# The low halves of all weights computed by VectorE alone

## The chip, the cores and the metric

The kernel runs on one core of one Trainium2 chip. The metric is the device time of one execution in microseconds (us); lower is better. The engines of the core have short names in the profile: PE is TensorE (PEld its weight loads), DVE is VectorE, ACT is ScalarE, POOL is GpSimd, SP issues the DMAs.

## The reference

One layer of a hybrid decoder, for a prompt of 2048 tokens and for 8 short sequences of 4 tokens that share the weights. All arrays are fp32, the model width is 1024:

```
h    = rmsnorm(x, norm1_g) * (1 + sc1) + sh1          # adaLN: sh, sc, g from silu(c) @ ada_w + ada_b
proj = h @ w_in                                       # columns split among three token mixers
mix  = concat(ssd(proj), rwkv7(proj), s5(proj)) @ w_out
x    = x + g1 * mix
h2   = rmsnorm(x, norm2_g) * (1 + sc2) + sh2
x    = x + g2 * (square(relu(h2 @ mlp_w1)) @ mlp_w2)  # 1024 -> 4096 -> 1024
y    = rmsnorm(x, final_g)
```

The mixers are a Mamba-2 SSD in chunks, an RWKV-7 time mixing and a complex-diagonal S5; their final states are outputs too. Only the four large products, with w_in, w_out, mlp_w1 and mlp_w2, use the weights that the change touches.

## The kernel before

Activations lie with features on the 128 partitions and tokens along the free axis. The prompt is cut into four blocks of 512 tokens (`NB`, `BT`); block `SB` = 2 carries the 32 sample tokens as 32 more columns. The input projection runs for all four blocks first; then, block by block, the output projection, and the MLP in chunks of four hidden tiles. The mixers' second stages are generators (`spawn`) that a planner (`pump`) fits between the matmuls, so most of the mixers' work lies beside the projections and the MLPs of blocks 0 and 1.

The large products keep fp32 accuracy by halves. TensorE multiplies in the rounded type fp32r, so each operand is split: a high half, the value rounded to fp32r, and a low half, the value minus its high half. A product is three matmuls per 128 x 128 weight block: high x high, high x low, low x high (the loop over `i` in `gemm` and `gemm2`). Accumulation is in a PSUM bank (`bk`).

The weights go through this stage by stage. `wload` brings a raw tile of 128 x 1024 into one of four buffers in `arena`. `wprep` lets ScalarE write the high half of 512 columns into a ring of four in `arena_r`; `wlow` writes the low half into the same slot of the ring: VectorE takes the first 512 - `WS.POOL` columns, GpSimd the other `WS.POOL`. `WS.POOL` is 288 (so 224 and 288 columns) for all input projections and for the output projection and MLP of blocks 0 and 1, and 0 from the output projection of block 2 on (line 2538). The first kind are the 176 halves of w_in and all but the last few of the 288 of blocks 0 and 1 in w_out, w1 and w2: the trace has 462. `whalf` and the middle of `gemm` (`k % 4 == 2`, one half ahead) call `wlow`, so the low half stands in VectorE's and GpSimd's queues among the mixers' instructions. Before each engine instruction stand the waits that the tile framework derives; each engine works through its queue in the order in which the program was written.

The order is written out by the program itself. Every instruction goes through `Eng.call` (line 198, which is why nearly all lines of the profile are L198), which issues it and then books it in `Plan`: `plan.run` moves the rough clock of its engine by an assumed cost (for a `tensor_tensor` of n columns, 72 + 1.04 n on VectorE and 60 + 2.4 n on GpSimd). `pump` looks at these clocks to choose which generator writes its next piece. GpSimd's other instructions are pieces of the mixers: subtractions and products of 504 or 512 columns and short copies.

Of the kernel before, what the change touches and what calls it, by code (L numbers as in the profile page):

```python
# [13 lines left out]
ALU = mybir.AluOpType  # L14
# [96 lines left out]


class Plan:
    """Rough clocks of the engines while the program is written; they only decide the order in which it is written."""

    LAT = {"PE": 197.0, "DVE": 128.0, "ACT": 143.0, "POOL": 85.0, "SP": 0.0}
    U = 32
# [130 lines left out]
def layer_kernel(ctx: ExitStack, tc: tile.TileContext, d, o, dbg=None):  # L248
    nc = tc.nc
    plan = Plan()  # L250
    V, S, P, T, Q = (Eng(plan, *x) for x in (("DVE", nc.vector), ("ACT", nc.scalar), ("POOL", nc.gpsimd), ("PE", nc.tensor), ("SP", nc.sync)))
# [31 lines left out]

    ctx.enter_context(tc.manual_schedule())

    # ------------------------------------------------------------ plumbing
    gens = []
    done = set()

# [146 lines left out]
    tt = V.tensor_tensor  # L436
# [11 lines left out]
    def bc(ap, k, n):  # L448
        return ap.unsqueeze(k).to_broadcast([*ap.shape[:k], n, *ap.shape[k:]])

    # ------------------------------------------------------------ constants
    cst = M.get(C_N)
    vec = M.get(V_N)
    cin = M1.get(72)
# [52 lines left out]
    s5dec = M.get(512)  # L507
    V.memset(s5h.f, 0.0)

    # ------------------------------------------------------------ small helpers  # L510
    def rsqrt(v, n, p=128):
        t_, y_, h_ = (grab(n, AM) for _ in range(3))
        t, y, h = t_.f[0:p], y_.f[0:p], h_.f[0:p]
        ts(t.bitcast(I32), v.bitcast(I32), 1, None, ALU.logical_shift_right)
        ts(h, v, -27.0 / 1024, None, ALU.mult)
        ts(y.bitcast(I32), t.bitcast(I32), -1.0, float(0x5F3759DF), ALU.mult, ALU.add)
        tt(t, y, y, ALU.mult)
        tt(t, t, v, ALU.mult)
        stt(t, t, -10.0 / 3, t, ALU.add, ALU.mult)
        yield 0  # L520
        stt(y, t, 5.0, y, ALU.add, ALU.mult)
        tt(t, y, y, ALU.mult)
        tt(t, t, h, ALU.mult)
        stt(y, t, 0.5625, y, ALU.add, ALU.mult)
        yield 0
        free(t_, h_)
        return y_
# [77 lines left out]
        ts(dv(D_A, 8), dv(D_A, 8), -1.0, None, ALU.mult)  # L605
        done.add("A")

    # ------------------------------------------------------------ adaLN
    mod = M.get(48 * 9)
    modv = mod.v("p (m s) -> p m s", m=48)  # L610
    G1 = M.get(72)
# [68 lines left out]
            yield  # L680
            yield from finish()

    # ------------------------------------------------------------ weights
    NWH = 4
    wring = [(MR.get(512), MR.get(512)) for _ in range(NWH)]
    wbuf = M.get(1024 * NRB)
# [3 lines left out]
    class WS:  # L690
# [4 lines left out]
        POOL = 288  # L695

    def wload(upto):
        while WS.loaded < min(upto, len(wseq)):
            i = WS.loaded
            dst = wraw[i % NRB]  # L700
            Q.dma_start(dst if wseq[i][1] != "oh" else dst.rearrange("p (m c) -> p m c", m=2), wseq[i][0])
            WS.loaded += 1

    def whalves(i):
        hi, lo = wring[i % NWH]
        return hi, lo, wraw[i // 2 % NRB][:, 512 * (i % 2):512 * (i % 2) + 512]
# [9 lines left out]
    def wlow(upto):  # L716
        while WS.low < min(upto, WS.ready):
            i = WS.low
            hi, lo, raw = whalves(i)
            c = 512 - WS.POOL  # L720
            tt(lo.r[:, 0:c], raw[:, 0:c], hi.f[:, 0:c], ALU.subtract)
            if c < 512:
                P.tensor_tensor(lo.r[:, c:], raw[:, c:], hi.f[:, c:], ALU.subtract)
            WS.low += 1
            wload(i // 2 + (NRB if i % 2 else NRB - 1))

    def whalf():
        i = WS.pos
        WS.pos += 1
        wprep(i + 3)  # L730
        wlow(i + 1)
        hi, lo = wring[i % NWH]
        return hi.r, lo.r
# [45 lines left out]
    def gemm(xs, hasS, drop=()):  # L779
        nk = len(xs)  # L780
        got, ws = [], []
        for (c0, c1) in pieces(hasS):
            bk = gbank()
            assert bk is not None
            n = c1 - c0
            cnt = 0
            for k in range(nk):
                if k % 4 == 0 and k // 4 == len(ws):
                    ws.append(whalf())
                if k % 4 == 2:  # L790
                    wlow(WS.pos + 2)
                hi, lo = ws[k // 4]
                xh, xl = xs[k]
                h_, l_ = hi[:, 128 * (k % 4):128 * (k % 4) + 128], lo[:, 128 * (k % 4):128 * (k % 4) + 128]
                for i, (w_, x_) in enumerate(((h_, xh), (h_, xl), (l_, xh))):
                    x_ = x_[:, c0:c1]
                    t = plan.when([w_, x_], "PE")
                    while t > plan.clk["PE"] + 150 and pump(t - plan.clk["PE"]):
                        pass
                    mm(bk[:, 0:n], w_, x_, start=cnt == 0, stop=cnt == nk * 3 - 1)  # L800
                    cnt += 1
                    if i == 2 and drop and c1 >= BT:
                        free(*drop[k])
                    if cnt % SLOT == 0 and cnt < nk * 3:
                        pump()
            got.append((bk, c0, c1))
        return got

    def gemm2(acts, hasS):
# [4 lines left out]
        for k in range(8):  # L814
            if k > 0 or not WS.pos:
                wait_for(lambda: len(acts) > k, "acts")
            if k == 0:
                pos = WS.pos
                wprep(pos + 2 * nt)
                wlow(pos + 2 * nt)  # L820
                WS.pos += 2 * nt
                wait_for(lambda: len(acts) > k, "acts")
            if k == 6:
                wprep(WS.pos + 1)
                wlow(WS.pos + 1)
            xh, xl = (x.r for x in acts[k])
            for u, (m, (c0, c1)) in enumerate(units):
                hi, lo = (w.r for w in wring[(pos + 2 * m + k // 4) % NWH])
                h_, l_ = hi[:, 128 * (k % 4):128 * (k % 4) + 128], lo[:, 128 * (k % 4):128 * (k % 4) + 128]
                for i, (w_, x_) in enumerate(((h_, xh), (h_, xl), (l_, xh))):  # L830
                    x_ = x_[:, c0:c1]
                    t = plan.when([w_, x_], "PE")
                    while t > plan.clk["PE"] + 150 and pump(t - plan.clk["PE"]):
                        pass
                    mm(bks[u][:, 0:c1 - c0], w_, x_, start=k + i == 0, stop=k == 7 and i == 2)
                    cnt += 1
                    if cnt % SLOT == 0 and cnt < 24 * len(units):
                        pump()
# [20 lines left out]
                fn(bk, BT - c0, c1 - c0, BT, True)  # L859
            gput(bk)  # L860

    # ------------------------------------------------------------ token mixers, first stage
    def store(dst, src):
        Q.dma_start(dst, src)

# [307 lines left out]
        ub.free()  # L1173
        done.add(("u", b, i))

    # ------------------------------------------------------------ S5
    LWS = -0.30326532985631671

    def s5_setup():
# [369 lines left out]
        yf.free()  # L1549
        done.add(("s5", b))  # L1550

    # ------------------------------------------------------------ SSD
    def ssd_chunk(b, c):
        smp = c == 4
        n = 32 if smp else 128
# [159 lines left out]
        for c in cs:  # L1715
            yield from admit(ssd_chunk(b, c), C_SSD, R_SSD(b))

    # ------------------------------------------------------------ RWKV, second stage
    def rw_pre(b):
        hasS = b == SB  # L1720
        nch = 9 if hasS else 8
# [370 lines left out]
        if b == SB:  # L2092
            spawn(ssd_gen(b, [4]), R_SMP)

    # ------------------------------------------------------------ main line
    def mix_flags(b):
        fl = [("s5", b)]
        for c in range(5 if b == SB else 4):
            fl += [("ssd", b, c), ("rw", b, c)]
        return fl  # L2100
# [403 lines left out]
        free(*xs)  # L2504
        done.add(("final", b))

    # ------------------------------------------------------------ run
    first4 = [4, 0, 5, 1, 6, 2, 7, 3]
    nxt = [[]]
    ys = []  # L2510
# [49 lines left out]
        dbg(nc, locals())  # L2560


# [1 line left out]
def _consts():  # L2564
    c = np.zeros((128, C_N), np.float32)
    i = np.arange(128)
    c[:, C_ID:C_ID + 128] = np.eye(128)
    c[:, C_MLE:C_MLE + 128] = i[:, None] <= i[None]
    c[:, C_MGT:C_MGT + 128] = i[:, None] > i[None]
    c[:, C_BD:C_BD + 128] = (i[:, None] // 64) == (i[None] // 64)  # L2570
    s, t = i[:, None] % 64, i[None] % 64
    c[:, C_GM:C_GM + 128] = np.where(i[None] < 64, s < t, s <= t)
    ok = (s < 32) & (t < 32) & (s // 4 == t // 4)
    c[:, C_GMS:C_GMS + 128] = ok & np.where(i[None] < 64, s < t, s <= t)
    j = np.arange(32)
    same = (j[:, None] // 4) == (j[None] // 4)
    c[:32, C_SMLE:C_SMLE + 32] = same & (j[:, None] <= j[None])
    c[:32, C_SMGT:C_SMGT + 32] = same & (j[:, None] > j[None])
    c[:, C_ONE] = 1
    c[:, C_HSEL:C_HSEL + 2] = (i[:, None] // 64) == np.arange(2)  # L2580
    c[:32, C_SSEL:C_SSEL + 8] = (j[:, None] // 4) == np.arange(8)
    c[:, C_RSEL:C_RSEL + 8] = ((i % 64)[:, None] < 32) & ((i % 64)[:, None] // 4 == np.arange(8))
    c[:, C_DTSEL:C_DTSEL + 8] = (i[:, None] % 32) == np.arange(8)
    c[:, C_S9:C_S9 + 9] = (i[:, None] % 32) == np.arange(9)
    return c
# [142 lines left out]
```

## Time and profile before

| | |
|---|---|
| runs | 2865.80, 2872.69, 2864.34 us (median 2865.8) |
| profiled execution | span 2863.7 us from the first to the last instruction; its device time is not listed beside it |
| PE busy | 2739.5 us, 96%, 16651 matmuls |
| DVE busy | 1967.3 us, 69%, 4567 instructions |
| ACT busy | 1142.5 us, 40% |
| POOL busy | 653.5 us, 23%, 829 instructions |
| DMA | 406.26 MB, mean 142 GB/s |
| mean granted clock of TensorE | 0.983 of full speed |

In a row of a group, the first number after the bar is the busy time in us, the second the mean duration of one instruction in ns, the third the engine's idle time ahead of it and what ended it. Tiles have the program's names: `arena` is plain fp32 memory, `arena_r` memory for fp32r (the halves), `bk` a PSUM bank. So `DVE TENSOR_TENSOR arena_r<-arena,arena_r 128x224` is VectorE's part of a weight's low half (raw minus high), and `POOL TENSOR_TENSOR arena_r<-arena,arena_r 128x288` GpSimd's part. The same with 512 columns on VectorE is a whole low half: of an activation, or, from block 2's output projection on, of a weight. A matmul's end is modelled, so a busy TensorE is not always one at its peak.

### The profile page before, as it was taken

The page shows a single profiled execution, that of the slowest core. Times are in us where ns is not written, and L with a number is a line of the kernel's source. Part 1 is how long each engine was busy: PE and PEld are TensorE (multiplying, and loading weights), DVE is VectorE, ACT ScalarE, POOL GpSimd, SP SyncE. Part 2 cuts the span into 40 slices and gives each one's busy share as a digit, 9 for nine tenths or more (in the row PEclk, how much of TensorE's full clock was granted, in tenths as well). Part 3 has the DMA queues.
Part 4 walks back from the last instruction along what each step waited for, and adds up shares of the span by engine and source line. Part 5 has one row for each costly group of instructions (what it writes and reads, how often), then busy time and mean ns, then how long its engine had stood idle before and what let it go on. Part 6 is the DMA issues. An engine that isn't in the chain of part 4 may idle for free.

```text
span 2863.7 us, 45369 instructions
## 1 busy us (share of the span) xinstructions
PE 2739.5 (96%) x16651; PEld 2265.7 (79%) x16651; DVE 1967.3 (69%) x4567; ACT 1142.5 (40%) x2153; POOL 653.5 (23%) x829
## 2 busy tenths in 40 slices
PE   7999889999999999999999999999999999999997
PEld 4677778877777777777777777778899999888886
DVE  6988996887997877666676778676653535643434
ACT  4354443454335432233443432334534344433342
POOL 1234432233442233322323343321000000000000
PEclk9999999999999999999999999999999999999999
DMA  8467656446553444433434364334222223232222
GB/s 284 155 213 252 201 163 198 164 155 215 170 191 115 144 125 155 146 115 97 159 129 135 118 188 142 120 118 151 96 89 89 89 89 133 82 126 96 99 93 74
DMA packets 302667, 406.26 MB, mean 142 GB/s; under 512 B 85604, under 2 KB 197348, under 8 KB 302444
## 3 DMA queue, kind: packets, MB, share of 16 engines
q1 hardware_dynamic: 302444, 403.36, 42.8%
q8 instruction: 131, 2.15, 0.3%
q14 instruction: 92, 0.75, 0.1%
HBM read 329.67 MB, written 73.62 MB: 141 GB/s over the span
## 4 chain that ended last, share of the span: by engine, by line
PE 62%; DVE 9%; issue 2%; ACT 1%; DMA 1%; POOL 0%; SPq 0%; DVEq 0%; POOLq 0%; ACTq 0%
PE bk L198 62%; DVE arena L198 7%; DVE arena_r L198 2%; ACT arena L198 1%; ACT arena_r L198 1%; DMA arena<-sph 0%; DMA arena<-spk 0%; POOL arena L198 0%; DMA arena<-in_w_out 0%; POOL arena_r L198 0%; DMA arena<-spl 0%; SPq L198 0%; DVEq L198 0%; DVEq L2724 0%; POOLq L198 0%
## 5 line engine op out<-in xcount | busy, mean ns | idle before, releaser
L198 PE MATMUL bk<-arena_r 128*128 128x512 f32 (+1 forms) x11344 | 2284.7, 358 | 61.7 <-DVE arena_r L198 41.5
L198 PEld LDWEIGHTS bk<-arena_r 128*128 128x128 f32 x11344 | 1843.9, 190 | 397.9 <-DVE arena_r L198 65.4
L198 DVE TENSOR_TENSOR arena_r<-arena,arena_r 128x224 fp32r<-128x224 f32 (+2 forms) x981 | 577.7, 610 | 416.9 <-ACT arena_r L198 410.6
L198 ACT ACTIVATE arena_r<-arena 128x512 fp32r<-128x512 f32 (+1 forms) x976 | 581.5, 627 | 468.4 <-PE bk L198 394.3
L198 POOL TENSOR_TENSOR arena_r<-arena,arena_r 128x288 fp32r<-128x288 f32 (+1 forms) x530 | 510.7, 976 | 1055.2 <-ACT arena_r L198 933.2
L198 ACT ACTIVATE arena<-bk 128x512 f32<-128x512 f32 (+8 forms) x619 | 271.9, 459 | 1008.5 <-PE bk L198 798.3
L198 PE MATMUL bk<-arena 128*128 128x128 f32 (+14 forms) x5139 | 540.3, 290 | 50.9 <-DVE arena L198 37.5
L198 PEld LDWEIGHTS bk<-arena 128*128 128x128 f32 (+6 forms) x5139 | 429.7, 152 | 179.7 <-issue 71.2
L198 DVE TENSOR_TENSOR arena<-arena 128x512 f32<-128x512 f32 (+16 forms) x1286 | 515.2, 411 | 51.1 <-ACT arena L198 16.6
L198 DVE SCALAR_TENSOR_TENSOR arena<-bk,arena 128x512 f32<-128x512 f32 (+1 forms) x368 | 235.4, 644 | 269.7 <-PE bk L198 264.0
L198 ACT ACTIVATE arena<-arena 128x512 f32<-128x512 f32 (+4 forms) x445 | 290.1, 664 | 208.1 <-DVE arena L198 189.7
L198 DVE SCALAR_TENSOR_TENSOR arena<-arena 128x512 f32<-128x512 f32 (+9 forms) x605 | 252.2, 430 | 26.6 <-ACT arena L198 6.7
L198 DVE TENSOR_TENSOR arena<-bk,arena 128x512 f32<-128x512 f32 (+4 forms) x277 | 101.2, 381 | 37.0 <-PE bk L198 31.4
L198 POOL TENSOR_TENSOR arena<-arena 128x512 f32<-128x512 f32 (+1 forms) x56 | 73.6, 1320 | 193.5 <-DVE arena L198 100.2
L198 DVE TENSOR_TENSOR arena<-arena,bk 128x512 f32<-128x512 f32 (+2 forms) x163 | 100.4, 627 | 15.3 <-PE bk L198 12.6
L198 DVE SCALAR_TENSOR_TENSOR arena<-arena,bk 64x64 f32<-64x64 f32 (+3 forms) x278 | 91.4, 355 | 27.4 <-PE bk L198 24.1
L198 DVE TENSOR_SCALAR arena<-arena 128x4 f32<-128x4 f32 (+14 forms) x359 | 95.8, 289 | 13.6 <-ACT arena L198 7.8
L198 POOL COPY arena<-arena 128x3 f32<-128x3 f32 (+6 forms) x222 | 70.0, 327 | 47.3 <-ACT arena L198 29.9
L198 ACT ACTIVATE arena<-bk,arena 128x512 f32<-128x512 f32 (+4 forms) x112 | 57.0, 535 | 17.8 <-PE bk L198 16.6
L198 DVE COPY arena<-bk 64x256 f32<-64x256 f32 (+5 forms) x85 | 43.6, 513 | 4.1 <-PE bk L198 2.6
L198 DVE TENSOR_TENSOR_SCAN arena<-arena 128x256 f32<-128x256 f32 (+2 forms) x40 | 36.1, 902 | 1.3
L198 DVE TENSOR_REDUCE arena<-arena 128x4 f32<-128x256 f32 (+1 forms) x34 | 14.0, 412 | 6.7 <-ACT arena L198 6.4
(14 smaller groups left out, 46.3 us busy)
## 6 DMA issues: line engine op xcount, KB each, us to landing
arena<-in_w SPq DMA_DIRECT2D x256, 512.0 KB
arena<-in_w_in SPq DMA_DIRECT2D x88, 512.0 KB
arena<-in_ada_w SPq DMA_DIRECT2D x24, 1024.0 KB
arena<-in_x SPq DMA_DIRECT2D x64, 256.0 KB
arena<-spk SPq DMA_DIRECT2D x32, 512.0 KB
arena<-in_w_out SPq DMA_DIRECT2D x32, 512.0 KB
spk<-arena SPq DMA_DIRECT2D x40, 256.0 KB
spl<-arena SPq DMA_DIRECT2D x33, 256.0 KB
```

Source lines behind the costliest of these rows:

```text
L198: r = fn(*a, **k)
```

## The change

VectorE computes the low half of all 512 columns in one instruction also where `WS.POOL` is 288. The two bookings of the planner stay as they were for the two pieces (same costs, same column ranges, in the same order), so that the order in which the program is written stays the same. GpSimd's subtraction is gone. Where `WS.POOL` is 0, the instruction is the one of before.

```diff
             c = 512 - WS.POOL
-            tt(lo.r[:, 0:c], raw[:, 0:c], hi.f[:, 0:c], ALU.subtract)
             if c < 512:
-                P.tensor_tensor(lo.r[:, c:], raw[:, c:], hi.f[:, c:], ALU.subtract)
+                op = "tensor_tensor"
+                nc.vector.tensor_tensor(lo.r, raw, hi.f, ALU.subtract)
+                plan.run("DVE", 72 + 1.04 * c, [lo.r[:, 0:c]], [raw[:, 0:c], hi.f[:, 0:c]], 0)
+                plan.run("POOL", 60 + 2.4 * (512 - c), [lo.r[:, c:]], [raw[:, c:], hi.f[:, c:]], 0)
+            else:
+                tt(lo.r, raw, hi.f, ALU.subtract)
             WS.low += 1
```

Beside it, comment lines and the docstring of `Plan` are left out of the file; line numbers ahead of the change stay.

## Rows read from the trace of the kernel before

**Rows 1.** Busy time (instructions) of each engine by stretch, granted clock, DMA share, GB/s:
```profile
0.00:1000.00 1000.00, 927.31 (x5854) 733.91 (x5855) 835.57 (x2048) 446.88 (x876) 334.50 (x471) 0.97 0.58 188
1000.00:2000.00 1000.00, 974.63 (x5684) 775.51 (x5684) 710.92 (x1654) 362.35 (x673) 318.98 (x359) 0.99 0.42 135
2040.00:2864.00 824.00, 802.12 (x4889) 724.10 (x4888) 396.81 (x805) 319.05 (x584) 0.00 (x0) 0.98 0.28 98
```

**Rows 2.** TensorE's waits, first 2000 us: total us, times, longest us:
```profile
PE bk L198 <- DVE arena_r L198: 39.7, 42, 3.9
PE bk L198 <- DVE arena L198: 34.3, 17, 13.8
PE bk L198 <- ACT arena_r L198: 9.3, 6, 3.6
PE bk L198 <- ACT arena L198: 6.9, 6, 1.7
...
PE bk L198 <- POOL arena_r L198: 0.7, 1, 0.7
```

**Rows 3.** The chain of waits from 677 us to the end, shares by line:
```profile
by line: PE bk L198 81.7%; DVE arena L198 9.6%; issue 3.0%; DVE arena_r L198 2.6%; ACT arena L198 0.8%; ACT arena_r L198 0.7%; DMA arena<-sph 0.2%; DMA arena<-spk 0.2%; POOL arena L198 0.2%; DMA arena<-in_w_out 0.2%; POOL arena_r L198 0.2%;
```

**Rows 4.** VectorE's groups by shape, 0 to 2000 us (columns as on the page):
```profile
L198 DVE TENSOR_TENSOR arena_r<-arena,arena_r 128x224 fp32r<-128x224 f32 x462 | 224.2, 489 | 120.8 <-ACT arena_r L198 116.0 <-DMA arena<-spg 3.1
L198 DVE SCALAR_TENSOR_TENSOR arena<-arena 128x512 f32<-128x512 f32 x176 | 146.6, 840 | 9.0 <-ACT arena L198 4.5 <-PE bk L198 0.9 <-POOL arena L198 0.8
L198 DVE SCALAR_TENSOR_TENSOR arena<-bk,arena 128x512 f32<-128x512 f32 x148 | 110.4, 746 | 99.2 <-PE bk L198 98.2
L198 DVE TENSOR_TENSOR arena<-arena 128x512 f32<-128x512 f32 x140 | 108.3, 776 | 2.6 <-ACT arena L198 0.7
L198 DVE TENSOR_TENSOR arena_r<-arena,arena_r 128x512 fp32r<-128x512 f32 x131 | 105.2, 809 | 38.1 <-ACT arena_r L198 37.5
L198 DVE TENSOR_TENSOR arena<-arena 128x256 f32<-128x256 f32 x155 | 75.9, 509 | 16.2 <-ACT arena L198 13.6
...
L198 DVE TENSOR_TENSOR arena<-arena 128x4 f32<-128x4 f32 x248 | 64.4, 267 | 9.2
```

**Rows 5.** The same groups of VectorE from 2040 us to the end:
```profile
L198 DVE TENSOR_TENSOR arena_r<-arena,arena_r 128x512 fp32r<-128x512 f32 x316 | 207.9, 685 | 224.9 <-ACT arena_r L198 224.5 <-issue 0.2
L198 DVE SCALAR_TENSOR_TENSOR arena<-bk,arena 128x512 f32<-128x512 f32 x72 | 53.9, 750 | 95.8 <-PE bk L198 95.8
...
L198 DVE SCALAR_TENSOR_TENSOR arena<-arena,bk 128x512 f32<-128x512 f32 x24 | 16.6, 741 | 5.5 <-PE bk L198 5.5
...
L198 DVE TENSOR_TENSOR arena<-arena 128x512 f32<-128x512 f32 x13 | 8.9, 686 | 0.5
...
L198 DVE TENSOR_TENSOR arena<-arena 128x4 f32<-128x4 f32 x12 | 2.0, 163 | 0.4
```

**Rows 6.** GpSimd's costliest groups by shape, whole span:
```profile
L198 POOL TENSOR_TENSOR arena_r<-arena,arena_r 128x288 fp32r<-128x288 f32 x462 | 436.3, 952 | 1037.0 <-ACT arena_r L198 933.2 <-PE bk L198 56.6 <-DMA arena<-in_x 17.4
L198 POOL TENSOR_TENSOR arena_r<-arena,arena_r 128x512 fp32r<-128x512 f32 x64 | 73.4, 1167 | 18.2 <-PE bk L198 18.2
L198 POOL TENSOR_TENSOR arena<-arena 128x512 f32<-128x512 f32 x40 | 47.5, 1193 | 139.5 <-PE bk L198 75.6 <-DVE arena L198 46.9 <-DMA arena<-in_w 7.1
L198 POOL TENSOR_TENSOR arena<-arena 128x504 f32<-128x504 f32 x16 | 26.1, 1637 | 53.9 <-DVE arena L198 53.3 <-PE bk L198 0.7
```

**Rows 7.** Timeline, 829 to 838 us: start, us, engine, what, [idle before]:
```profile
831.39 4.32 POOL L198 TENSOR_TENSOR arena_r<-arena,arena_r 128x288 fp32r<-128x288 f32 x4
...
831.90 1.45 DVE L198 TENSOR_TENSOR arena<-arena 128x4 f32<-128x4 f32 x2
...
834.80 1.81 DVE L198 TENSOR_TENSOR arena<-arena 128x4 f32<-128x4 f32 x6
...
836.53 0.38 DVE L198 TENSOR_TENSOR arena_r<-arena,arena_r 128x224 fp32r<-128x224 f32 x1
...
836.97 1.65 PE L198 MATMUL bk<-arena_r 128*128 128x512 f32 x3 [3.94 <-DVE arena_r L198]
```

## The prediction

> **What bounds the kernel now.** I read the page's totals first and then, as an average over stages says little, the busy time by stretch. TensorE is marked busy for 927 + 975 + 802 of 2824 us, 96%. VectorE (DVE) is busy for 836 of the first 1000 us, for 711 of the second, and for 397 of 824 after 2040 us, where GpSimd (POOL), before that at 335 and 319, does nothing at all [rows 1]. So VectorE is close to its limit only where GpSimd works too. The waits of TensorE up to 2000 us name the same engine: 39.7 us before matmuls whose operands in arena_r (the halves) VectorE wrote, 34.3 us on VectorE's writes to arena, of which one wait of 13.8 us is the very first matmul's, and 0.7 us on GpSimd's halves [rows 2]. Without that first one, VectorE ends 39.7 + 34.3 - 13.8 = 60.2 us of TensorE's idle time. The chain of waits from 677 us on (it can't be followed further back) is 81.7% TensorE, 9.6 + 2.6 = 12.2% VectorE, 1.5% ScalarE, 0.2% GpSimd for each of its two arenas [rows 3]. TensorE sets the end, and what can be won or lost lies where it waits for VectorE, all of it before 2040 us.
>
> **What is removed and added.** 462 GpSimd subtractions of 288 columns, 952 ns each and 436 us together, go [rows 6]. The 462 VectorE subtractions of 224 columns, 489 ns each [rows 4], become 512 columns wide. The trace has that very instruction where GpSimd is idle: 316 times, 685 ns [rows 5]. Added VectorE time: 462 x (685 - 489) = 90.6 us. ScalarE's high halves, the loads and the order of the queues stay; the planner still books the two old pieces, so the written program has the same order. From the output projection of block 2 on the subtraction was whole before, so nothing changes there.
>
> **What VectorE gets back.** Compare the same instruction with GpSimd at work (before 2000 us) and without (after 2040 us). Instructions that read two SBUF tiles are longer beside GpSimd: 512 columns into arena_r 809 against 685 ns, 512 columns in arena 776 against 686, four columns 267 against 163. One that reads a PSUM bank and arena is not: 746 against 750 [rows 4, 5]. The single instruction shows it best: near 832 us GpSimd runs four of its subtractions back to back for 4.32 us, and two four-column VectorE instructions in that time take 1.45 us instead of 2 x 0.163 [rows 7]. VectorE stands still while GpSimd works, and then does its own work at full speed.
> The sum over the stretch up to 2000 us: 140 x 90 ns = 12.6 us; 131 x 124 = 16.2; 248 x 104 = 25.8; the 176 scalar_tensor_tensor on arena, 840 against 741 for the nearest row without GpSimd (one operand in PSUM), 99 x 176 = 17.4; the 155 of 256 columns, 509 against some 422 (an estimate, on the line between 163 ns for 4 and 686 for 512 columns), 13.5 [rows 4, 5]. Together 85.5 us in 500 us of busy time, 17%. VectorE is busy for 1546 us in this stretch [rows 1]; less these 500 and the 224 of the low halves, 822 us are left, of which the PSUM readers gain nothing. I count half of them at 17%, an estimate: 70 us. (Bounds: none, and 140 for all.) So GpSimd costs the rest of VectorE's work some 155 us. Not all of it is due to the removed instructions: of the four costly tensor_tensor groups of GpSimd, 436.3 of 583.3 us are theirs, 75% [rows 6]. The remaining groups go on blocking. 155 x 0.75 = 116 us come back.
> Net VectorE time: 90.6 - 116 = -25 us. Bounds: +27 us if only the five groups gain (85.5 x 0.75 = 64), -78 us if all the rest gains and for the same 75% (225 x 0.75 = 169).
> The Trainium skill (SBUF — State Buffer, section "SBUF: two separate sides") gives a reason for such rows: GpSimd and a VectorE instruction with two SBUF inputs take one port pair as an exclusive lock for a whole instruction. By that rule every wait behind a removed instruction goes wholly, and my sum stands, with the waits behind GpSimd's other groups left.
>
> **What of it reaches the end.** VectorE's time counts only where TensorE waits for it. The stall that ends at 836.97 us is such a place: TensorE idles 3.94 us for a low half that VectorE issues at 836.53 as soon as it is through its queue. Ahead of it stand eight four-column instructions of 1.45 and 1.81 us where 8 x 0.163 would do, so 1.95 us of waiting, nearly all under the four GpSimd subtractions; the low half itself becomes 0.30 us longer (685 for 380 ns) [rows 5, 7]. Net 1.65 of 3.94 us, 42%. If the 60.2 us [rows 2] shrink alike: 25 us. That is all of the net 25 us of VectorE's time, which is plausible because VectorE is blocked most where its queue is full. From below: nothing reaches the end, if each stall's next-late is as late (ScalarE's high half, or the PSUM eviction before it). From above: all 60.2 us. I take 24 us.
> Other effects. A low half is ready when the later of its two halves is; TensorE hardly ever waits for GpSimd's part (0.7 us), so dropping it brings nothing by itself [rows 2]. Where no GpSimd instruction collides, the low half is 0.30 us later than now; behind it in VectorE's queue stand the PSUM evictions (746 ns each), and for those TensorE waits only when banks run out. The cover is TensorE's backlog; gone, each of the 462 costs 0.30 us, which the on-path share of 12.2% turns into 462 x 0.30 x 0.122 = 17 us of loss at most; I leave it out of the sum beyond the net above, and in the range. GpSimd's other work (120 tensor_tensor and short copies) no longer queues behind a subtraction that waits for ScalarE; no waits of weight are on it (0.2% of the chain), so 0, with some 5 us of gain as the other end [rows 3]. The clock is at 0.97 of full speed in the first 1000 us and 0.99 in the second [rows 1], some 40 us at the higher level lost; part of it follows the stalls. I count 0 and keep up to 10 us of gain for the low end.
>
> **Sum.** The profiled execution: span 2863.7 us; its time with what lies around it is not listed, the three runs (median 2865.8) lie 0.6 us and more above the span. 2863.7 - 24 = 2840, and the 2 us to the median: 2842 us.
>
> **Rivals.** (1) Hidden: VectorE's relief lands where TensorE has work in its queue, and stalls end by the next-late engine. For it: TensorE 96% busy, and VectorE is only 12.2% of the chain. Against: VectorE ends most of TensorE's idle time, ScalarE 9.3 + 6.9 us before 2000 [rows 2]. Time: 2866, within 2857 to 2874.
> (2) Slower: the long VectorE instructions have another cause than GpSimd, so that the waiting stays with VectorE while its work grows. Then the 512-column low half takes what this instruction takes in this stretch today, 809 ns, and nothing else gets shorter: 462 x (809 - 489) = 148 us. VectorE, at 836 of 1000 us, has no room for it in the first half; at the share of VectorE on the chain, 0.122, it costs 18 us, at twice that share, as the chain leaves out the busiest 677 us, 36: some 2893. It decides from the point where a low half takes on average over 489 ns with no other group relieved, or over 489 + 116/462 = 740 ns with the relief counted above. Against: PSUM readers don't lengthen, and instructions of 4 columns lengthen by as much as those of 512 (104 and 90 to 124 ns) [rows 4, 5].
> The Trainium skill (Perfetto Trace Analysis, section "Optimizing Scalar/DVE Operations") speaks for this side in one sentence, as it advises moving work off a saturated VectorE, and GpSimd is named as a place; and against it in the next, as the two share a port and moving work between them may not help. The rows at 832 us side with the second.
> (3) More: all stalls behind VectorE close and some clock comes back: 2866 - 60 = 2806.
>
> **Chances.** Forecast (2815 to 2857) 0.60; more than that 0.06; hidden 0.21; slower 0.13. About 0.3%, 8.6 us, is what a measurement of this kernel can tell from no change. So faster 0.66, same 0.21, slower 0.13. The range 2808 to 2877 leaves out most of the slower case and the end of the third.
>
> **What would show it.** After: 462 more VectorE subtractions of 512 columns near 700 ns and none of 224; four-column instructions near 190 ns; VectorE's busy time up to 2000 us 1490 to 1545 us (now 1546); TensorE's waits for VectorE down by a third or more before 2000 us, and the part from the output projection of block 2 on as long as now. Wrong if the low halves stay near 800 ns, if VectorE's total rises by over 50 us, or if TensorE's waits only change name, to ScalarE.

## The result, and the profile after

The changed kernel takes 2826.9 us (median of 4 runs, 2826.5 to 2832.2) against 2867.4 us for the kernel before in the same comparison: a ratio of 0.9857, with a 95% interval of 0.984 to 0.9875. It is faster by 41 us. Its profiled execution is the slowest of the four: 2832.2 us, a span of 2830.1. So the two traces differ by 2863.7 - 2830.1 = 33.6 us, and the medians by some 7 us more; a second trace of the same kernel, below, has a span of 2824.7.

The totals of the page after: VectorE is busy for 1936.0 us, 31.3 us less than before, though it has taken over what GpSimd did.

```profile
PE 2729.6 (96%) x16651; PEld 2264.7 (80%) x16651; DVE 1936.0 (68%) x4567; ACT 1141.2 (40%) x2153; POOL 227.8 (8%) x367
```

VectorE's groups by shape, up to 1965 us, the same point of the program as 2000 us before (shape, count, busy us, mean ns, idle before):

```profile
L723 DVE TENSOR_TENSOR arena_r<-arena,arena_r 128x512 fp32r<-128x512 f32 x462 | 328.0, 715 | 119.3 <-ACT arena_r L198 113.7 <-DMA arena<-spg 3.1 <-DMA arena<-sph 1.7
L198 DVE SCALAR_TENSOR_TENSOR arena<-arena 128x512 f32<-128x512 f32 x176 | 133.4, 765 | 9.7 <-ACT arena L198 4.5 <-POOL arena L198 2.4
L198 DVE SCALAR_TENSOR_TENSOR arena<-bk,arena 128x512 f32<-128x512 f32 x148 | 110.4, 747 | 94.1 <-PE bk L198 92.3 <-DMA arena<-in_x 0.9
L198 DVE TENSOR_TENSOR arena<-arena 128x512 f32<-128x512 f32 x140 | 98.7, 707 | 2.3 <-ACT arena L198 0.9
L198 DVE TENSOR_TENSOR arena_r<-arena,arena_r 128x512 fp32r<-128x512 f32 x130 | 91.2, 708 | 39.3 <-ACT arena_r L198 38.6
L198 DVE TENSOR_TENSOR arena<-arena 128x256 f32<-128x256 f32 x155 | 68.4, 460 | 21.5 <-ACT arena L198 16.0 <-issue 2.9
...
L198 DVE TENSOR_TENSOR arena<-arena 128x4 f32<-128x4 f32 x248 | 47.9, 200 | 9.5 <-DVE arena L198 0.5
```

Row by row beside [rows 4]: the whole low half takes 715 ns where the part of 224 columns took 489. Everything else that reads two SBUF tiles is shorter: 840 to 765, 776 to 707, 809 to 708, 509 to 460, and the four-column instruction 267 to 200. The reader of a PSUM bank stays at 747 (746). None comes quite down to [rows 5]: GpSimd's other work is still there. When e9, below, takes 64 of GpSimd's products away too, the low half falls to 695 ns and the four-column instruction to 190.

TensorE's waits to the same point, beside [rows 2]:

```profile
PE bk L198 <- DVE arena L198: 31.4, 15, 14.2
PE bk L198 <- DVE arena_r L723: 17.1, 19, 3.4
PE bk L198 <- ACT arena_r L198: 8.8, 6, 3.9
PE bk L198 <- ACT arena L198: 8.7, 8, 2.0
...
PE bk L198 <- DVE arena_r L198: 3.1, 4, 2.5
```

The waits for halves that VectorE wrote fall from 39.7 to 17.1 + 3.1 us; those for `arena`, which hold the wait at the start, hardly (34.3 to 31.4), and ScalarE's stay.

To see where the time went, one needs a mark that stands at the same place of both programs. The first load of w_out, issued in the last part of the input projections, is one. In the trace before, and after:

```profile
785.81 0.38 SPq L198 DMA_DIRECT2D arena<-in_w_out  x1
```

```profile
755.81 0.47 SPq L198 DMA_DIRECT2D arena<-in_w_out  x1
```

Busy time and granted clock from the start to that mark, and from there to the end (columns as in [rows 1]), before:

```profile
0.00:785.81 785.81, 721.98 (x4675) 573.81 (x4676) 658.89 (x1651) 352.35 (x703) 268.87 (x401) 0.97 0.60 197
785.81:2863.70 2077.89, 2017.54 (x11977) 1691.90 (x11976) 1308.44 (x2917) 790.16 (x1450) 384.62 (x428) 0.99 0.37 121
```

and after:

```profile
0.00:755.81 755.81, 710.75 (x4675) 567.18 (x4676) 627.76 (x1644) 351.72 (x703) 107.53 (x227) 0.99 0.63 205
755.81:2830.10 2074.29, 2018.81 (x11977) 1697.52 (x11975) 1308.22 (x2923) 789.45 (x1450) 120.27 (x140) 0.98 0.38 121
```

Of the 33.6 us, 30.0 lie ahead of the mark: 785.8 to 755.8 us. VectorE's busy time falls there by 31.1 us, from 659 to 628; behind the mark it is the same, 1308.4 and 1308.2: there the longer low halves cost VectorE what they give back. The stretch is still shorter by 3.6 us, 2077.9 to 2074.3, and that has its place. Two more marks are the first loads of w_out for block 1 and for block 2, the ninth and the seventeenth of 32. Between these two, before, after, and in e8 and e4, which are explained below:

```profile
1374.49:1940.02 565.53, 546.87 (x3036) 433.37 (x3035) 413.50 (x941) 208.32 (x378) 193.94 (x228) 0.99 0.43 138
```

```profile
1346.90:1906.10 559.20, 545.51 (x3036) 434.98 (x3036) 412.97 (x940) 208.32 (x378) 67.81 (x82) 0.99 0.44 139
```

```profile
1378.55:1937.16 558.61, 544.45 (x3036) 433.81 (x3036) 413.73 (x940) 208.34 (x378) 68.35 (x82) 0.99 0.43 140
```

```profile
1338.50:1907.02 568.52, 550.02 (x3036) 435.75 (x3035) 414.69 (x941) 208.45 (x378) 194.01 (x228) 0.98 0.42 137
```

The two kernels with 288 columns on GpSimd here (before and e4) take 565.5 and 568.5 us, the two without 559.2 and 558.6, while VectorE's total hardly differs (413.0 to 414.7). So 6 to 10 us come back in this stretch, though not through VectorE's total. By what else isn't shown; a GpSimd instruction as such isn't it, as e3, with 144 columns on GpSimd, takes 559.4 us there. From the first mark to the second it is 588.7 us before and 591.1 after, and from the third to the end 923.7 and 924.0.

### The profile page after: what moved, and what is told of

Its sections match the earlier page's. It is cut to its first block, busy times and chain, and to the rows that moved or that the text cites. A ratio compares the mean times of both kernels' runs of the same rounds, so it can differ in the third digit from the quotient of the medians.

```text
span 2830.1 us, 44425 instructions
## 1 busy us (share of the span) xinstructions
PE 2729.6 (96%) x16651; PEld 2264.7 (80%) x16651; DVE 1936.0 (68%) x4567; ACT 1141.2 (40%) x2153; POOL 227.8 (8%) x367
## 4 chain that ended last, share of the span: by engine, by line
PE 57%; DVE 6%; ACT 1%; issue 1%; DMA 0%; SPq 0%; POOL 0%; DVEq 0%; ACTq 0%; POOLq 0%
PE bk L198 57%; DVE arena L198 4%; DVE arena_r L198 1%; DVE arena_r L723 1%; ACT arena L198 1%; ACT arena_r L198 1%; DMA arena<-spc 0%; SPq L198 0%; POOL arena L198 0%; DMA spl<-arena 0%; DMA arena<-spg 0%; DVEq L198 0%; DVEq L2728 0%; DVEq L723 0%; ACTq L198 0%
## 5 line engine op out<-in xcount | busy, mean ns | idle before, releaser
L198 PE MATMUL bk<-arena_r 128*128 128x512 f32 (+1 forms) x11344 | 2273.5, 357 | 38.9 <-DVE arena_r L723 17.1
L198 DVE TENSOR_TENSOR arena_r<-arena,arena_r 128x512 fp32r<-128x512 f32 (+1 forms) x519 | 345.5, 690 | 296.3 <-ACT arena_r L198 294.9
L198 DVE TENSOR_TENSOR arena<-arena 128x512 f32<-128x512 f32 (+16 forms) x1286 | 444.8, 357 | 58.2 <-ACT arena L198 19.3
L723 DVE TENSOR_TENSOR arena_r<-arena,arena_r 128x512 fp32r<-128x512 f32 x462 | 328.0, 715 | 119.3 <-ACT arena_r L198 113.7
L198 DVE SCALAR_TENSOR_TENSOR arena<-arena 128x512 f32<-128x512 f32 (+9 forms) x605 | 226.3, 387 | 21.9 <-ACT arena L198 5.3
L198 DVE TENSOR_TENSOR arena<-arena,bk 128x512 f32<-128x512 f32 (+2 forms) x163 | 100.5, 628 | 13.9 <-PE bk L198 11.0
L198 POOL TENSOR_TENSOR arena_r<-arena,arena_r 128x512 fp32r<-128x512 f32 (+1 forms) x68 | 81.8, 1223 | 255.0 <-PE bk L198 254.9
L198 DVE TENSOR_SCALAR arena<-arena 128x4 f32<-128x4 f32 (+14 forms) x359 | 77.3, 238 | 13.5 <-ACT arena L198 7.8
```

The source lines that it names most:

```text
L198: r = fn(*a, **k)
L723: nc.vector.tensor_tensor(lo.r, raw, hi.f, ALU.subtract)
```

## Experiments

Theory A: GpSimd's instructions stop VectorE for as long as they run; the change took 462 of them away, and where VectorE's queue is full, the time that VectorE gets back is the kernel's. Rival B: a low half no longer waits for GpSimd's part. Rival C: GpSimd's other work had to wait behind subtractions that wait for ScalarE. All kernels have the changed kernel's order, but for e7_replanned. The diffs are cut: the declaration of the scratch tile `scr` and the planner's two bookings, which stay, aren't shown.

**e1_pool_dummy288.** The blocking back, without a matmul that waits for it:

```diff
                 nc.vector.tensor_tensor(lo.r, raw, hi.f, ALU.subtract)
+                nc.gpsimd.tensor_tensor(scr, raw[:, c:], hi.f[:, c:], ALU.subtract)
```

> The changed kernel, with GpSimd still subtracting its 288 columns at the same places, but into a scratch tile that nobody reads. Theory A (GpSimd's two-input instructions block VectorE, and that is what the change took away): the blocking is back and VectorE keeps the longer low halves, so it is worse off than before by up to 462 x 0.30 = 139 us; in the first 800 us, where VectorE is full, that is some 180 x 0.30 = 54 us of path: 2895 to 2940 us. Rival B (the gain is that the low half no longer waits for GpSimd's part): nobody waits for the scratch, so the time stays at 2827. Rival C (the gain is GpSimd's other work, which stood in its queue behind subtractions that wait for ScalarE): that queue is back, nothing else: about 2867.

2943.4 us, a ratio of 1.0261 (1.0237 to 1.0285) to the kernel before, 3 us above the range of A. Nobody reads the scratch, so B, which left the time at 2827, can't account for this, and C can't make it slower than before. ScalarE does wait for the new instruction, which reads what ScalarE overwrites next: 24 us in all. But in e2 it waits for 27 us, and there the gain stays. The rows of VectorE's groups, up to the same point of the program, show the stretching back, now on 512 columns:

```profile
L724 DVE TENSOR_TENSOR arena_r<-arena,arena_r 128x512 fp32r<-128x512 f32 x462 | 356.2, 776 | 105.3 <-ACT arena_r L198 102.9 <-PE bk L198 1.1
...
L198 DVE TENSOR_TENSOR arena<-arena 128x4 f32<-128x4 f32 x248 | 62.7, 260 | 9.7 <-DVE arena L198 0.7
```

Up to the mark and behind it:

```profile
0.00:827.30 827.30, 735.71 (x4674) 583.82 (x4675) 710.99 (x1646) 352.07 (x703) 293.21 (x401) 0.96 0.57 187
827.30:2944.00 2116.70, 2039.95 (x11979) 1704.11 (x11977) 1397.60 (x2922) 789.63 (x1450) 414.33 (x428) 0.98 0.36 119
```

Against the trace after, VectorE has 83 us more ahead of the mark and the stretch is 71 us longer; behind it, 89 us more and 42 us longer.

**e2_pool_dummy16.** The same with 16 columns: the same order and the same waits in GpSimd's queue, almost no blocking.

```diff
+                nc.gpsimd.tensor_tensor(scr[:, 0:16], raw[:, 496:512], hi.f[:, 496:512], ALU.subtract)
```

> As e1_pool_dummy288, but the scratch subtraction has 16 columns instead of 288: it waits for ScalarE at the same places in GpSimd's queue, and is over in some 0.2 us. Theory A: blocking is nearly gone: 2828 to 2842 us. Rival B: 2827. Rival C: the order of GpSimd's queue and its waits are as before the change: about 2867.

2830.8 us, 0.9868 (0.9846 to 0.989): the gain stays. C falls. Together with e1 this says that what counts is how long GpSimd's instruction runs, not that it is there.

**e3_split144** and **e12_split144_scratch.** 144 columns on GpSimd, and the same load without the wait for it. e12 writes GpSimd's part to the scratch tile and leaves the last 144 columns of these low halves at zero:

```diff
-                nc.vector.tensor_tensor(lo.r, raw, hi.f, ALU.subtract)
+                nc.vector.tensor_tensor(lo.r[:, 0:368], raw[:, 0:368], hi.f[:, 0:368], ALU.subtract)
+                nc.gpsimd.tensor_tensor(lo.r[:, 368:], raw[:, 368:], hi.f[:, 368:], ALU.subtract)   # e3; to scr in e12
```

> VectorE takes 368 of 512 columns, GpSimd 144. Theory A: blocking time and VectorE's work both move about halfway, so the time lies about halfway: 2840 to 2855 us. Rival B: GpSimd's part still gates the low half: 2860 to 2867. If a balance between the two engines pays at all, this is where it would be better than 2827.

> As e3_split144, but GpSimd writes its 144 columns to a scratch tile and the last 144 columns of each low half of those 462 are left out (the ring holds zeros there): the same load on both engines, and no matmul waits for GpSimd. e3_split144 was 17 us longer than the changed kernel up to the first load of w_out with only 8 us more VectorE time. If that is the wait for GpSimd's part (rival B, in part): this stage falls from 768 to about 759 us or less. If it is the blocking alone: 764 to 770 us.

e3 takes 2833.2 us (ratio 0.9882, 0.9861 to 0.9903), nearer to the changed kernel than halfway, and under the range of A. VectorE's total is that of the changed kernel (636.2 + 1300.1 us below, against 1936.0). Its low halves of 368 columns take 586 ns, so 462 x (715 - 586) = 60 us saved are blocked away again. For 288 columns the same reckoning gives 104 + 31 = 135 us, so half the columns block somewhat less than half as much. e12 takes 2835.3 us (0.9883). The low halves of e3:

```profile
L722 DVE TENSOR_TENSOR arena_r<-arena,arena_r 128x368 fp32r<-128x368 f32 x462 | 268.8, 586 | 126.3 <-ACT arena_r L198 124.9 <-issue 0.3
```

To the mark and behind it, e3 and then e12:

```profile
0.00:768.06 768.06, 715.63 (x4677) 570.73 (x4678) 636.16 (x1647) 351.96 (x703) 225.73 (x401) 0.98 0.61 201
768.06:2836.20 2068.14, 2014.60 (x11976) 1693.32 (x11974) 1300.13 (x2921) 789.79 (x1450) 307.61 (x428) 0.99 0.37 122
```

```profile
0.00:764.07 764.07, 713.63 (x4674) 568.62 (x4675) 637.44 (x1647) 352.03 (x703) 226.15 (x405) 0.98 0.62 202
764.07:2833.20 2069.13, 2017.82 (x11978) 1694.94 (x11976) 1300.78 (x2921) 790.17 (x1450) 307.23 (x428) 0.99 0.37 122
```

Ahead of the mark e12 is 4 us shorter than e3, no more than two executions of one kernel differ there (755.8 and 751.3, below). So B isn't shown even as a part; 4 us of it can't be excluded. The same test with 288 columns wasn't run; there the trace before has 0.7 us of TensorE's waiting for GpSimd's halves [rows 2].

**e4_w_in_only** and **e8_all_but_w_in.** The change for the 176 halves of w_in alone, and for the other 286 alone:

```diff
-                nc.vector.tensor_tensor(lo.r, raw, hi.f, ALU.subtract)
+                if i < 2 * NB * (NWIN - 1):      # e4; e8: >=
+                    nc.vector.tensor_tensor(lo.r, raw, hi.f, ALU.subtract)
+                else:
+                    nc.vector.tensor_tensor(lo.r[:, 0:c], raw[:, 0:c], hi.f[:, 0:c], ALU.subtract)
+                    nc.gpsimd.tensor_tensor(lo.r[:, c:], raw[:, c:], hi.f[:, c:], ALU.subtract)
```

> The change only for the 176 halves of w_in (up to some 930 us); the other 286 stay split as before. Theory A, with VectorE's queue as the path: the gap between the two traces opens from 60 to 810 us, where VectorE is full, and by 30 of the 34 us: 2833 to 2842 us. A rival by which each low half brings the same (a shorter wait, one semaphore less): 176 of 462 parts, 38%, so 2850 to 2855.

> The complement of e4_w_in_only: the 176 halves of w_in split as before, the other 286 whole on VectorE. Theory A: beyond 930 us VectorE has room, so only the few stalls between 1500 and 2000 us gain: 2852 to 2863 us, and the gains of the two add up to the 40 us of the full change. By an equal share for each half: 286 of 462, 62% of 40 us: 2842.

e4: 2837.2 us, 0.9896 (0.9873 to 0.992), 28 us under the kernel before. e8: 2861.1 us, 0.9972 (0.9959 to 0.9986), 8.7 us under it. Most of the gain is w_in's, and the two parts (28 + 9) make up the whole within a few us. The marks tell them apart. In e4 the first mark falls at 749.0 us and the rest takes 2082.1; in e8 the mark is at 786.6, as late as before, and the rest takes 2073.1. The profiled span of e8 is 4.0 us under the one before. e8's profile has VectorE's total as before (1966.9 us), so A in its plain form gives it nothing. Its gain lies between the marks of block 1 and block 2, 558.6 us against 565.5 (above), and 3 us of it are paid in the stretch before that, 591.9 against 588.7. Why that stretch gets shorter with the same VectorE total stays open.

**e5_pool_copy400.** GpSimd reads one tile instead of two:

```diff
+                nc.gpsimd.tensor_copy(scr, hi.f[:, 0:400])
```

> The changed kernel, with a GpSimd copy of 400 columns of each high half into a scratch tile that nobody reads, at the places where the subtraction stood: GpSimd is busy for some 0.6 us at each place, but reads one SBUF tile instead of two. If any GpSimd instruction that reads SBUF blocks VectorE, the blocking per us is that of e1_pool_dummy288 (174 us of VectorE's time for 473 us of GpSimd's), some 100 us: 2880 to 2905 us. If only those that read two tiles block: 2825 to 2835 us.

2871.4 us, 1.0004 (0.999 to 1.0018): between the two ranges, so both were mis-sized. A copy blocks too. At 486.97 us it runs for 0.52 us, and two four-column VectorE instructions there take 0.68 us instead of 2 x 0.163 [rows 5]; later, two copies in a row:

```profile
486.83 0.68 DVE L198 TENSOR_TENSOR arena<-arena 128x4 f32<-128x4 f32 x2
486.97 0.52 POOL L725 CAST scr<-arena_r 128x400 fp32r<-128x400 f32 x1 [12.55 <-ACT arena_r L198]
```

```profile
830.78 1.50 POOL L725 CAST scr<-arena_r 128x400 fp32r<-128x400 f32 x2
831.32 0.99 DVE L198 TENSOR_TENSOR arena<-arena 128x4 f32<-128x4 f32 x2
```

VectorE's total rises by 82 us over the changed kernel's, the span by 2871.8 - 2830.1 = 42. I had scaled by GpSimd's records, and that was too much. In e1 473 us of them cost VectorE 2108.6 - 1936.0 = 173 us, 0.36 us per us; here 337 us cost 82, only 0.24. The records average 0.73 us where the shortest copy takes 0.51, so they may hold GpSimd's own waiting; but by the shortest records, 0.78 and 0.51 us, the copy is still the cheaper one (0.48 and 0.35). Why isn't shown.

**e6_dve_extra140.** VectorE time without GpSimd:

```diff
+                nc.vector.tensor_tensor(scr[:, 0:140], raw[:, 0:140], hi.f[:, 0:140], ALU.subtract)
```

> The changed kernel, with a VectorE subtraction of 140 columns into a scratch tile behind each of the 462 low halves: 462 x 0.30 = 139 us more VectorE time, without any GpSimd instruction. Theory A, by which VectorE's time is what the blocking costs: the same 139 us as e1_pool_dummy288 had over the kernel before, so about the same step, some +78 us: 2890 to 2915 us. Rival (the blocking hurts by what it delays, the low halves, more than by VectorE's time): at most +35 us, 2830 to 2862.

2890.0 us, 1.0074 (1.0051 to 1.0097), at the lower end of A's range and far above the rival's. The 462 extra instructions show 334 ns each, but VectorE's total rises by 108 us only, as records of neighbours overlap:

```profile
L725 DVE TENSOR_TENSOR scr<-arena,arena_r 128x140 fp32r<-128x140 f32 x462 | 154.3, 334 | 0.0
```

Up to the mark and behind it:

```profile
0.00:782.66 782.66, 722.10 (x4676) 573.72 (x4677) 668.60 (x1817) 352.87 (x703) 108.74 (x227) 0.97 0.61 197
782.66:2896.50 2113.84, 2042.19 (x11977) 1708.42 (x11975) 1375.77 (x3212) 790.76 (x1450) 121.43 (x140) 0.97 0.36 119
```

41 us more VectorE time make the first stretch 27 us longer than in the trace after, 68 us the second 40.

**e7_replanned.** `WS.POOL = 0` throughout, so that the planner books whole low halves.

```diff
-        POOL = 288
+        POOL = 0
...
-        WS.POOL = 0 if b > 1 else 288
+        WS.POOL = 0
```

> The kernel before with WS.POOL = 0 throughout: whole low halves on VectorE as in the changed kernel, but booked as such by the planner, so the order of the program is another. Theory A has VectorE's total as in the changed kernel (1936 us) and so 2815 to 2845 us, with the sign of the difference to 2827 open. If the kept order carries the gain: 2850 us or more.

2835.7 us, 0.9883 (0.9867 to 0.9898): the gain doesn't hang on the kept order, and the new order is not better, though VectorE's total is 1924.8 us. TensorE's granted clock is lower in it, 0.978 to 0.979 in its four executions against 0.985 to 0.986 in the changed kernel's.

**e9_masks_on_scalar**, with **e10_changed_again** beside it. GpSimd's largest remaining group on ScalarE:

```diff
-                P.tensor_tensor(Rv[k], bc(mle, 1, 4), bc(src[:, 4 * g:4 * g + 4], 2, n), ALU.mult)
+                if smp:
+                    P.tensor_tensor(Rv[k], bc(mle, 1, 4), bc(src[:, 4 * g:4 * g + 4], 2, n), ALU.mult)
+                else:
+                    for h in range(4):
+                        nc.scalar.activation(Rv[k][:, h], mle, AF.Identity, scale=src[:, 4 * g + h:4 * g + h + 1])
```

> The changed kernel, with GpSimd's largest remaining group, the 64 products of a mask with a column of scalars (128x512 into arena_r, 79 us, the most blocking that is left), as 4 ScalarE instructions of 128 columns each, in the kept order. Theory A: some 29 us of VectorE's waiting go, but only the part before 810 us, some 10 us, is on the path, and ScalarE gets 256 instructions, 60 to 80 us at 40% busy: 2815 to 2830 us. If ScalarE's added work delays the high halves and the PSUM evictions: 2830 to 2850 us.

> The changed kernel itself, unaltered, beside e9_masks_on_scalar on the same chip: a ratio to the kernel before of 0.984 to 0.9875, and times that spread over some 6 us, as the four executions so far did.

e10: 2827.1 us, 0.9854 (0.9838 to 0.987), the result again; its profiled span, 2824.7 us, is 39.0 under the one before:

```profile
0.00:751.30 751.30, 707.31 (x4672) 566.08 (x4673) 628.04 (x1647) 350.90 (x703) 107.11 (x227) 0.99 0.63 206
751.30:2824.70 2073.40, 2019.59 (x11980) 1697.12 (x11979) 1309.00 (x2921) 789.89 (x1450) 119.67 (x140) 0.98 0.37 121
```

e9: 2831.4 us, 0.9871 (0.9853 to 0.9889), not faster, though VectorE's total falls to 1908.8 us. That is in the range for the case that ScalarE's added work delays other things. The 256 ScalarE instructions take 78 us, as expected, and VectorE's instructions come nearly down to [rows 5], the low half to 695 ns; but the low halves wait longer for ScalarE, 134.9 us against 113.7 in the first table of groups above:

```profile
L1582 ACT ACTIVATE arena_r<-arena,arena_r 128x128 fp32r<-128x128 f32 x256 | 78.1, 392 | 0.0
```

```profile
L723 DVE TENSOR_TENSOR arena_r<-arena,arena_r 128x512 fp32r<-128x512 f32 x462 | 318.9, 695 | 138.9 <-ACT arena_r L198 134.9 <-DMA arena<-spg 3.1
...
L198 DVE TENSOR_TENSOR arena<-arena 128x4 f32<-128x4 f32 x248 | 45.5, 190 | 9.5 <-DVE arena L198 0.5
```

Up to the mark and behind it:

```profile
0.00:762.15 762.15, 715.01 (x4671) 570.92 (x4672) 617.63 (x1649) 376.68 (x791) 78.15 (x205) 0.98 0.62 203
762.15:2834.00 2071.85, 2020.57 (x11981) 1698.49 (x11979) 1291.16 (x2918) 837.40 (x1618) 68.46 (x98) 0.98 0.37 121
```

Ahead of the mark VectorE has 10 us less than in e10, yet the stretch is 11 us longer, with 26 us more of ScalarE; behind it, 18 us less of VectorE bring nothing measurable (2071.9 against 2073.4 us).

**e11_w_in_whole_rest144.** The best form of each stage, by the profiles of e3 and e10: e4's `if`, with 368 and 144 columns in the `else`.

> Low halves of w_in whole on VectorE, the other 286 split with 144 columns on GpSimd. Up to the first load of w_out the whole form was the shortest (751 us against 768 with 144 columns and 786 with 288), behind it the split of 144 (2068 against 2073 and 2078 us of profiled span). If the two stages add up: 751 + 2068 = 2819 of span, 2821 us, 5 to 6 us under the changed kernel. If the 5 us behind are scatter: 2825 to 2830.

2832.1 us, 0.9862 (0.9841 to 0.9884); one run of four was at 2821.7, the other three at 2831.7 to 2832.6. It is above both ranges, and so not shown to be better. No version tried is shown to beat the changed kernel.

## Why the prediction was right, and where it was too small

Forecast 2842 us, measured 2826.9; the direction and the mechanism were right, the gain was 41 us where I expected 24.

- The added VectorE time: 462 x (685 - 489) = 90.6 us forecast, 462 x (715 - 489) = 104 us measured. The base of 685 ns is from a stretch without any GpSimd work; here GpSimd's other groups still block the low halves (695 ns in e9, where the largest of them is gone).
- The relief: the five groups give 176 x 75 + 140 x 69 + 130 x 101 + 155 x 49 + 248 x 67 ns = 60 us, forecast 64. The rest of VectorE gives 104 + 31.3 - 60 = 75 us, forecast 52; as the five groups got back 60 of 85.5 us, 70% where I took 75%, it was rather the half that I counted as gaining that was too little. Net -31.3 us, forecast -25.
- From VectorE's time to the end, one term came out as forecast and one was missing. I priced the stalls by TensorE's idle rows and took 42% of 60.2 us. TensorE's idle time over the whole span (span less busy time) falls from 124.2 to 100.5 us, by 23.7, where I took 24. But its marked busy time falls too, from 2739.5 to 2729.6 us, and together that is the 33.6 us between the traces; the other 7 of the 41 us are the executions that were profiled. Up to the mark, TensorE's waits for VectorE, without the first matmul's, fall from 22.2 + 29.4 - 13.8 = 37.8 to 6.2 + 25.8 - 14.2 = 17.8 us, more than half. Before, and after:

```profile
PE bk L198 <- DVE arena L198: 29.4, 10, 13.8
PE bk L198 <- DVE arena_r L198: 22.2, 21, 3.2
```

```profile
PE bk L198 <- DVE arena L198: 25.8, 9, 14.2
PE bk L198 <- DVE arena_r L723: 6.2, 11, 1.2
```

But the stretch is shorter by 30.0 us. TensorE's idle time there (stretch less busy time) falls by 18.8 us, from 63.8 to 45.1; the other 11.2 us come out of its marked busy time, 722.0 to 710.8, with the same 4675 matmuls. This part does not stand in the idle rows. The granted clock of the stretch rises from 0.97 to 0.99, which I had counted as 0 with up to 10 us as the other end. The thirteen traces with the kept order bear on it: up to the mark, TensorE's marked busy time runs from 706 us (e4, clock 0.99) to 736 us (e1, clock 0.96), but busy time times granted clock is 698 to 706 us in all of them (700 before, 704 after). So the marked busy time goes with the clock, by enough for all of the 11.2 us. What moves the clock is not shown, as no run here changed it alone; on the whole it is lower in the traces in which this stretch is longer.
- That the 42% of one stall came near the 38% by which all of them shrank (last point) is luck: that very stall hardly shrank, from 3.94 to 3.42 us. GpSimd's next group, the mask products, moved up into the gap and blocks the same two instructions, now for 1.93 us where it was 1.45 [rows 7]:

```profile
801.47 2.42 POOL L198 TENSOR_TENSOR arena_r<-arena,arena_r 128x512 fp32r<-128x512 f32 x2
801.98 1.93 DVE L198 TENSOR_TENSOR arena<-arena 128x4 f32<-128x4 f32 x2
...
805.56 0.68 DVE L723 TENSOR_TENSOR arena_r<-arena,arena_r 128x512 fp32r<-128x512 f32 x1
...
806.30 0.96 PE L198 MATMUL bk<-arena_r 128*128 128x512 f32 x3 [3.42 <-DVE arena_r L723]
```

- "Wholly hidden" fell: ahead of the mark 31 us of VectorE's time were worth 30 us, in e10 31 and 35. "Slower" fell by its own criterion: a low half takes 715 ns, under the 740 from which it would have decided. The Trainium skill's advice to move work off a saturated VectorE (Perfetto Trace Analysis, section "Optimizing Scalar/DVE Operations") does not hold here with GpSimd as the place: where VectorE was fullest, doing those 288 columns itself made its total smaller by 31 us. The next sentence there, that the two share a port and that moving work between them might not help, agrees with the runs.
- What was to show it came: whole low halves near 700 ns (715), four-column instructions near 190 ns (200), VectorE's busy time up to 2000 us between 1490 and 1545 us (1514, to 1965 us), the part from block 2's output projection on as long as before (923.7 and 924.0 us), and TensorE's waits for VectorE down by a third (from 60.2 to 31.4 + 17.1 + 3.1 - 14.2 = 37.4 us, 38%).

## What to carry to other kernels

Before work is split between VectorE and GpSimd, look for the same VectorE instruction with and without GpSimd beside it: if readers of two SBUF tiles lengthen and readers of PSUM don't, GpSimd's time is taken out of VectorE's. Then price a change by the stage in which VectorE's queue is full, as here one us of VectorE was worth 0.65 to 1 us of the kernel up to the mark (e6, e1, the change) and some half behind it (e6, e1), with block 1 as the exception, where time came back without VectorE's total. And price a stall by the length of its stretch and the granted clock in it, not by TensorE's idle rows alone.

## What the runs showed of the hardware

A GpSimd copy, with one tile read, blocks VectorE like a subtraction with two: 0.52 us of copy made 0.68 us out of two instructions of 0.163 us. The Trainium skill (SBUF — State Buffer, section "SBUF: two separate sides") names any GpSimd instruction that reads SBUF as the other party of the lock, and these rows agree. GpSimd's own records vary as well: 16 columns show 423 ns on average in e2 and 211 at the shortest, 288 columns 1024 ns in e1 and 784 at the shortest. That they hold GpSimd's waiting for VectorE would fit, but isn't shown. Two executions of the same program differed by 4.5 us at the mark (755.8 and 751.3 us) and by 0.9 us from there to the end.
